# Splitting an expert's gated rows earlier, and another order for the last norm, in an expert layer on one core

## The chip, the cores and the metric

The kernel runs on one core of a Trainium2 chip. The metric is the device time of that core for one execution, in microseconds (us). A core has TensorE (PE, matrix products, with its weight loads shown as PEld), VectorE (DVE), ScalarE (ACT), GpSimd (POOL) and SyncE (SP, which here issues the transfers). Each has its own list of instructions and runs it in order; semaphores hold one back until another has delivered. The time is that of the last core to end, here the only one.

## The reference, cut to what matters

The input is 256 tokens of width 1024 in float32. Two layers are computed: retention and a dense SwiGLU, then stick-breaking attention and an expert SwiGLU. The change touches only the expert layer and the norm behind it:

```python
def moe_swiglu(x, w_router, w_in, w_out):          # 256 tokens, 8 experts, hidden width 3584
    logits = (xt @ w_router).astype(jnp.float32)
    top_val, top_idx = lax.top_k(logits, 2)
    top_w = jax.nn.softmax(top_val, axis=-1)
    gates = sum over the 2 choices of one_hot(top_idx) * top_w
    for e in range(8):
        y = y + gates[:, e:e + 1] * swiglu(xt, w_in[e], w_out[e])
...
# every sub-layer: x <- layer_norm(alpha * x + f(x)); here f is the experts' sum
```

where `swiglu(x, w_in, w_out)` splits `x @ w_in` into gate and up and gives `(silu(gate) * up) @ w_out`.

## The kernel before, in words

Up to about 530 us run the retention layer, the dense SwiGLU, the attention and the router; nothing in them changes but line numbers. Then come the eight experts, where the change lies.

An expert works only on the tokens that chose it, up to CAP = 96 rows in three groups of 32. A one-hot matrix (L801) selects them, and a matmul with it (`pgx`, L817) gathers them, transposed, into `xg` (L826). The hidden width of 3584 is worked in two units: u = 0 with 2048 columns, u = 1 with 1536. For each unit the order in the code (`experts`) is: the gate projection (`gemm_e`, matmuls on L1102), its Silu on ScalarE (L1173), at u = 1 the work between experts (below), the up projection, the product with up (L1192) and its transpose (L1194) on VectorE, and then the down projection of the unit before this one (`down`). So the down projection that finishes an expert's rows runs in the next expert's u = 0, behind that unit's gate and up.

When an expert's rows are finished, `rows_of` copies them out of PSUM (`po`) into `y`: twelve copies of 32x256, the eight of the first two groups on ScalarE and the four of the third on VectorE. They are kept in `done`. The work between experts comes at the next u = 1, after the gate: `scatter` multiplies the rows by their gates and adds them to the residual `xa`. Because TensorE takes the rounded type fp32r, the gated rows are split in two parts: `yh` (ScalarE, L1155) is the gated row rounded, `yl` (VectorE, L1156) what the rounding lost. For each half of the columns (n) and each half of the tokens (t), two matmuls with the transposed one-hot matrix `gT` (L1159 with `yh`, L1160 with `yl`) put the rows in their places, and VectorE adds the result (L1161). Behind it `slots` prepares `gT` and the gates `gs` of the expert in work (transposes and products on TensorE into `pgt`, L1085 and L1087, copies on ScalarE), and the next expert's rows are gathered. Then follows the up projection.

The third group of 32 rows is worked last in a branch that TensorE alone takes (`by_need`), since some experts have at most 64 rows.

All expert weights stream from memory through fourteen 1 MB buffers (`raw`). SyncE issues the load of a buffer (L213) when TensorE has read it for the last time, in the order in which TensorE takes them; at most eight are on their way. Nothing else sets the order: it is the order of the code on each engine, with semaphores between.

After the last expert come its down projection, `scatter` once more, this time with the sums of the norm behind each addition (`stats`, L477), and then a test whether any expert had more than 96 rows (`tc.If(most[0] > CAP)`, L1227). If so, a second pass of all experts runs, several thousand instructions that lie in the program between the test and what follows; with these inputs it isn't taken, and every engine jumps over it. Behind it the last norm: the sums are combined (`mv`, L455), GpSimd computes the reciprocal of the deviation (`rs`, L456 and L457) and `nmr` (L484); for the tokens t = 0 VectorE subtracts the mean (L488, `centre`) and scales (L492, `scale`), for t = 1 ScalarE normalises (L498) and the gain and bias (L502, L503, `affine`) are applied by GpSimd to the first half of the columns and by VectorE to the second. SyncE stores four blocks (L1235).

## Time and profile before

| what | us |
|---|---|
| three runs | 1427.40, 1422.75, 1426.74 (median 1426.74) |
| the profiled execution's own time | 1422.93 |
| its span, first to last instruction | 1421.1 |
| mean granted TensorE clock, share of full speed | 0.974 |
| TensorE busy | 1349.7 (95%) |
| VectorE, ScalarE, GpSimd busy | 443.4, 314.2, 58.5 |

The profiled execution lasts 1.8 us longer than its span. Its own time is 3.8 us below the median of the three runs. Times in rows are us from the start of the span. [...] A line number is that of the kernel before unless the text says otherwise; the changed file's lines stand one to seven further down.

### The profile page before, as it was taken

The numbers are of one execution on the slowest core, as the hardware profiler recorded it, in microseconds if no ns is written. First come the engines' busy times: TensorE is split into PE (matmuls) and PEld (weight loads), VectorE is DVE, ScalarE is ACT, GpSimd is POOL, SyncE is SP. The second block draws the span as 40 slices with busy tenths as digits, with TensorE's granted clock in tenths as the row PEclk, the third lists the DMA queues.
The fourth block names the chain that finished last, engine by engine and source line by source line (L and its number), as shares of the span: only waits on it lengthen the run. The fifth ranks groups of instructions, "written<-read, shape, count | busy, mean of one in ns | idle before, by whom it ended". The sixth has DMA issues, their size and how long they took to land. (4 is left out here: it accounts for less than half of the span.)

```text
span 1421.1 us, 29884 instructions
## 1 busy us (share of the span) xinstructions
PE 1349.7 (95%) x13608; PEld 842.3 (59%) x13608; DVE 443.4 (31%) x617; ACT 314.2 (22%) x466; POOL 58.5 (4%) x80
## 2 busy tenths in 40 slices
PE   9999999999999999987989999999999999999894
PEld 7888879999989863533524444454444453443442
DVE  6746667555566570101201200200200200200204
ACT  5544425444447520001000000100100100100101
POOL 0212110000010020000000000000000000000001
PEclk9999999999999999999999999999999999999997
DMA  9864536655586356999999999989999999999960
GB/s 338 296 210 151 175 119 238 205 180 182 144 243 241 139 223 202 406 418 412 411 419 412 412 418 410 405 341 413 411 418 413 411 402 414 411 418 414 412 271 33
DMA packets 137251, 447.36 MB, mean 315 GB/s; under 512 B 9088, under 2 KB 56976, under 8 KB 120720
## 3 DMA queue, kind: packets, MB, share of 16 engines
q1 hardware_dynamic: 136144, 442.01, 80.9%
q0 software_dynamic: 960, 3.15, 0.7%
q8 instruction: 122, 2.00, 0.6%
q14 instruction: 25, 0.20, 0.0%
HBM read 444.08 MB, written 1.05 MB: 313 GB/s over the span
## 5 line engine op out<-in xcount | busy, mean ns | idle before, releaser
L1102 PE MATMUL pe<-raw,xg 128*32 128x512 f32 (+1 forms) x5304 | 513.3, 543 | 21.4 <-DMA raw<-in_moe_w_in_dram 9.6
L1102 PEld LDWEIGHTS pe<-raw,xg 128*32 128x32 f32 x5304 | 185.5, 110 | 339.6 <-issue 305.3
L1102 PE MATMUL po<-raw,hT 128*32 128x256 f32 x4544 | 249.9, 379 | 5.8 <-DMA raw<-in_moe_w_out_dram 3.3
L265 DVE TENSOR_TENSOR w<-raw,w 128x1024 fp32r<-128x1024 f32 x162 | 198.1, 1234 | 143.8 <-ACT w L264 139.8
L1102 PEld LDWEIGHTS po<-raw,hT 128*32 128x32 f32 x4544 | 158.0, 110 | 100.8 <-issue 7.4
L264 ACT CAST w<-raw 128x1024 fp32r<-128x1024 f32 x162 | 168.2, 1047 | 134.3 <-issue 32.1
L1192 DVE TENSOR_TENSOR hs<-hs,pe 128x512 f32<-128x512 f32 (+1 forms) x48 | 29.1, 620 | 384.0 <-PE pe L1102 382.6
L1173 ACT ACTIVATE hs<-pe 128x512 f32<-128x512 f32 (+1 forms) x48 | 25.4, 543 | 507.5 <-PE pe L1102 507.5
L393 PE MATMUL pf<-xT_h,w 128*128 128x256 f32 x448 | 126.9, 283 | 0.0
L395 PE MATMUL pf<-xT_l,w 128*128 128x256 f32 x448 | 126.2, 282 | 0.0
L394 PE MATMUL pf<-xT_h,w 128*128 128x256 f32 x448 | 126.1, 281 | 0.0
L1194 DVE STREAM_TRANSPOSE hT<-hs 128x512 f32<-128x512 f32 (+1 forms) x48 | 27.2, 617 | 230.0 <-PE po L1102 125.0
L393 PEld LDWEIGHTS pf<-xT_h,w 128*128 128x128 f32 x448 | 84.4, 188 | 0.3
L394 PEld LDWEIGHTS pf<-xT_h,w 128*128 128x128 f32 x448 | 84.4, 188 | 0.3
L395 PEld LDWEIGHTS pf<-xT_l,w 128*128 128x128 f32 x448 | 84.4, 188 | 0.0
L1146 ACT COPY y<-po 32x256 f32<-32x256 f32 x64 | 23.3, 364 | 258.4 <-PE po L1102 257.7
L456 POOL TENSOR_SCALAR rs<-mv 128x1 f32<-128x1 f32 x16 | 5.6, 350 | 1292.4 <-DVE mv L455 1284.5
L368 PE MATMUL pv<-w,xT_l 128*128 128x512 f32 x96 | 38.4, 400 | 0.0
L369 PE MATMUL pv<-w,xT_h 128*128 128x512 f32 x96 | 37.9, 395 | 0.0
L370 PE MATMUL pv<-w,xT_h 128*128 128x512 f32 x96 | 37.9, 395 | 0.0
L1156 DVE SCALAR_TENSOR_TENSOR yl<-y,gs,yh 96x512 fp32r<-96x512 f32 x16 | 11.9, 744 | 82.9 <-ACT yh L1155 82.8
L393 PE MATMUL pq<-xT_h,w 128*128 128x256 f32 x128 | 36.3, 283 | 0.0
(208 smaller groups left out, 1274.1 us busy)
## 6 DMA issues: line engine op xcount, KB each, us to landing
raw<-in_moe_w_in_dram SPq DMA_DIRECT2D x128, 1024.0 KB, 18.9
raw<-in_moe_w_out_dram SPq DMA_DIRECT2D x112, 1024.0 KB, 18.4
raw<-in_moe_w_in_dram SPq DMA_DIRECT2D x128, 768.0 KB, 15.2
raw<-in_ret_w_in_dram SPq DMA_DIRECT2D x22, 1024.0 KB, 9.1
raw<-in_ffn_w_in_dram SPq DMA_DIRECT2D x20, 1024.0 KB, 5.1
raw<-in_ffn_w_out_dram SPq DMA_DIRECT2D x11, 1024.0 KB, 5.0
raw<-in_ret_w_out_dram SPq DMA_DIRECT2D x8, 1024.0 KB, 5.0
raw<-in_sb_w_kv_dram SPq DMA_DIRECT2D x4, 1024.0 KB, 5.3
```

Of the source, the lines that this page charges most:

```text
L264: nc.scalar.copy(hv, v)
L265: nc.vector.tensor_sub(lv, v, hv.bitcast(F32))
L368: nc.tensor.matmul(o, sl, mh, start=first, stop=False)
L369: nc.tensor.matmul(o, sh, mh, start=False, stop=False)
L370: nc.tensor.matmul(o, sh, ml, start=False, stop=last)
L393: nc.tensor.matmul(o, lo[:, k, :], xT_h[:, k, :], start=(k == 0), stop=False)
L394: nc.tensor.matmul(o, h[:, k, :], xT_h[:, k, :], start=False, stop=False)
L395: nc.tensor.matmul(o, h[:, k, :], xT_l[:, k, :], start=False, stop=(k == KD - 1))
L1102: nc.tensor.matmul(ov, lhs[r], w, start=first and not (shared and r == 1), stop=last, skip_group_check=True)
L1173: nc.scalar.activation(hs[:, r, :], pg[r], AF.Silu)
L1192: nc.vector.tensor_mul(hs[:, r, :], hs[:, r, :], pu[r])
L1194: nc.vector.transpose(hT[:, r].rearrange("p k s -> p (k s)"), hs[:, r, :])
```

## The change

The split into `yh` and `yl` moves from `scatter` into `rows_of`, so it is issued right behind the copies of the finished rows; each of its four results has a tile of its own (t0 to t3), where two tiles were used twice before. The copies of the third group alternate between ScalarE and VectorE. The reciprocal deviation of the last norm is computed ahead of the test, for t = 0 first. The branch gets a label, and an announcement of its likely outcome is issued on all engines but TensorE ahead of the last down projection. In the last norm GpSimd applies no gain and bias any more: VectorE does it for both halves of t = 1, behind the scaling of t = 0, and ScalarE's normalisation is issued first.

```diff
--- before.py
+++ after.py
@@ -18,6 +18,7 @@
 AX = mybir.AxisListType
 PSUM = bass.MemoryType.PSUM
 PE = mybir.EngineType.PE
+ENGINES = [getattr(mybir.EngineType, e) for e in ("Activation", "DVE", "PE", "Pool", "SP")]
 
 P = 128
 S = 256
@@ -1138,26 +1139,28 @@
         a, b = wtile("po"), wtile("po")
         return [a[:, :256], a[:, 256:], b[:, :256]]
 
-    def rows_of(po):
+    def rows_of(po, gs):
 
         y = mp2.tile([P, D], F32, tag="y", name=nm("y"))
         for r in range(NB):
             for c in range(4):
-                (nc.scalar.copy if r < 2 else nc.vector.tensor_copy)(
+                (nc.scalar.copy if r < 2 or c % 2 == 0 else nc.vector.tensor_copy)(
                     y[r * 32:(r + 1) * 32, c * 256:(c + 1) * 256], po[r][c * 32:(c + 1) * 32])
-        return y
-
-    def scatter(y, gT, gs, norm=None):
-
+        out_ = []
         for n in range(2):
-            yh = mp.tile([P, 512], FR, tag="t0", name=nm("yh"))[:CAP]
-            yl = mp.tile([P, 512], FR, tag="t1", name=nm("yl"))[:CAP]
+            yh, yl = [mp.tile([P, 512], FR, tag=f"t{2 * n + i}", name=nm("y"))[:CAP] for i in range(2)]
             nc.scalar.activation(yh, y[:CAP, half(n)], AF.Copy, scale=gs[:CAP])
             nc.vector.scalar_tensor_tensor(yl, y[:CAP, half(n)], gs[:CAP], yh.bitcast(F32), OP.mult, OP.subtract)
+            out_.append((yh, yl))
+        return out_
+
+    def scatter(rows, gT, norm=None):
+
+        for n in range(2):
             for t in range(2):
                 p = wtile("psc")
-                nc.tensor.matmul(p, gT[:CAP, t, :], yh, start=True, stop=False)
-                nc.tensor.matmul(p, gT[:CAP, t, :], yl, start=False, stop=True)
+                for i in range(2):
+                    nc.tensor.matmul(p, gT[:CAP, t, :], rows[n][i], start=(i == 0), stop=(i == 1))
                 nc.vector.tensor_add(xa[:, t, half(n)], xa[:, t, half(n)], p)
                 if norm is not None:
                     norm[t].stats(n)
@@ -1197,12 +1200,16 @@
                         po = new_po()
                     down(s, *pend[0], po, pend[1] == 0, pend[1] == 1, third[e - (u == 0)])
                     if pend[1] == 1:
-                        done = (rows_of(po), *sl)
+                        done = (rows_of(po, sl[1]), sl[0])
                 pend = ((hT, n // P), u)
             if e + 1 < NE:
                 xg = nxt
+        if most is not None:
+            tc.mark_branch_hint_location("more", 0, engines=[e for e in ENGINES if e != PE])
         down(s, *pend[0], po, False, True, third[NE - 1])
-        scatter(rows_of(po), *sl, norm)
+        scatter(rows_of(po, sl[1]), sl[0], norm)
+        for t in range(2):
+            norm[t].rstd(t == 1)
 
     norm = [Norm(t, [], xa[:, t, :]) for t in range(2)]
     for t in range(2):
@@ -1224,7 +1231,7 @@
         g = one_hot(0, pos)
         experts(st2, pos, g, gather(g), norm)
 
-    with tc.If(most[0] > CAP):
+    with tc.If(most[0] > CAP, label="more"):
         more(p2)
         with tc.If(most[0] > 2 * CAP):
             nc.vector.tensor_scalar(p2, p2, float(CAP), None, OP.subtract)
@@ -1234,17 +1241,14 @@
     def store(t, n):
         nc.sync.dma_start(out[0, t * P:(t + 1) * P, half(n)], xa[:, t, half(n)])
 
-    for t in (1, 0):
-        norm[t].rstd(t == 1)
+    norm[1].normalise(0, 1)
     for n in range(2):
         norm[0].centre(n)
-    norm[1].normalise(0, 1)
-    norm[1].affine(0, nc.gpsimd, nc.gpsimd)
     for n in range(2):
         norm[0].scale(n)
         store(0, n)
-    norm[1].affine(1, nc.vector, nc.vector)
-    for n in (1, 0):
+    for n in range(2):
+        norm[1].affine(n, nc.vector, nc.vector)
         store(1, n)
```

On ScalarE, at the rows of the last expert but one (`po` holds the finished rows, `hs` is the next unit's Silu, `pgt` what `slots` computed), the program before has:

```order
L1146 COPY y_11626<-po_11015 32x256 [waits PE_49]
L1146 COPY y_11626<-po_11015 32x256 x7
L1173 ACTIVATE hs_11639<-pe_11640 128x384 [waits DVE_49,PE_49]
L1118 UNCONDITIONAL_BRANCH
L1173 ACTIVATE hs_11639<-pe_11641 128x384 [waits PE_49]
L1173 ACTIVATE hs_11639<-pe_11642 128x384 [waits PE_49]
L1155 ACTIVATE yh_11759<-y_11626,gs_10857 96x512 [waits DVE_49,Activation_49]
L1155 ACTIVATE yh_11771<-y_11626,gs_10857 96x512 [waits DVE_49,PE_49]
L1090 CAST gT_11788<-pgt_11783 128x256 [waits PE_49]
L1092 COPY gs_11790<-pgt_11783 128x1 [waits DVE_49]
```

and the changed program has, where the two split results `yh` are both named `y`:

```order
L1147 COPY y_11626<-po_11015 32x256 [waits PE_49]
L1147 COPY y_11626<-po_11015 32x256 x7
L1147 COPY y_11626<-po_11016 32x256 [waits PE_49]
L1147 COPY y_11626<-po_11016 32x256 [waits DVE_49]
L1152 ACTIVATE y_11639<-y_11626,gs_10857 96x512 [waits Activation_49]
L1152 ACTIVATE y_11643<-y_11626,gs_10857 96x512 [waits DVE_49]
L1176 ACTIVATE hs_11647<-pe_11648 128x384 [waits PE_49]
L1119 UNCONDITIONAL_BRANCH
L1176 ACTIVATE hs_11647<-pe_11649 128x384 [waits PE_49]
L1176 ACTIVATE hs_11647<-pe_11650 128x384 [waits PE_49]
L1091 CAST gT_11788<-pgt_11783 128x256 [waits PE_49]
L1093 COPY gs_11790<-pgt_11783 128x1 [waits DVE_49]
```

The two multiplications with the gates stood behind the three Silus of the next u = 1 and waited there for `yl` of the earlier half and for TensorE; they now follow the copies, ahead of the Silus, and two copies more stand in front of them.

On GpSimd, from the load of the largest row count to the end (`nmax` is that count, `x_87` and the like earlier tiles of the residual, `neghalf` the exponent), the program before has:

```order
L1181 TENSOR_LOAD nmax [waits DVE_49]
L1227 COMPARE_AND_BRANCH
L1229 COMPARE_AND_BRANCH
L1229 UNCONDITIONAL_BRANCH x2
L1227 UNCONDITIONAL_BRANCH
L456 TENSOR_SCALAR rs_27137<-mv_27136 128x1 [waits DVE_49]
L457 TENSOR_TENSOR rs_27137<-rs_27137,neghalf 128x1 [waits Pool_49]
L484 TENSOR_SCALAR nmr_27141<-mv_27136,rs_27137 128x1 [waits Pool_49]
L456 TENSOR_SCALAR rs_27144<-mv_27143 128x1 [waits DVE_49]
L457 TENSOR_TENSOR rs_27144<-rs_27144,neghalf 128x1 [waits Pool_49]
L502 TENSOR_TENSOR xa<-xa,gbt 128x512 [waits DMAHW5_49,Activation_49]
L503 TENSOR_TENSOR xa<-xa,gbt 128x512 [waits DMAHW7_49,Pool_49]
```

and the changed program, up to its jump:

```order
L1184 TENSOR_LOAD nmax [waits DVE_49]
L457 TENSOR_SCALAR rs_12293<-mv_12292 128x1 [waits DVE_49]
L458 TENSOR_TENSOR rs_12293<-rs_12293,neghalf 128x1 [waits Pool_49]
L457 TENSOR_SCALAR rs_12298<-mv_12297 128x1 [waits DVE_49]
L458 TENSOR_TENSOR rs_12298<-rs_12298,neghalf 128x1 [waits Pool_49]
L485 TENSOR_SCALAR nmr_12302<-mv_12297,rs_12298 128x1 [waits Pool_49]
L1234 COMPARE_AND_BRANCH
```

Before, the jump came right behind the load of the count, long ahead of the end, and the five instructions of the norm behind it. Now the five stand between the load and the jump, and nothing of GpSimd's follows the jump in the path that is taken.

## Rows read from the trace of the kernel before

**Rows 1.** Waits, whole span: engine, line, waited for; us in total, times, longest.

```profile
PE psc L1159 <- ACT yh L1155: 15.7, 16, 1.8
...
PE psc L1160 <- DVE yl L1156: 6.2, 16, 1.6
...
PE pe L1102 <- DMA raw<-in_moe_w_in_dram: 9.6, 15, 2.0
```

**Rows 2.** Page part 2, slices of 35.5 us: memory traffic.

```profile
GB/s 338 296 210 151 175 119 238 205 180 182 144 243 241 139 223 202 406 418 412 411 419 412 412 418 410 405 341 413 411 418 413 411 402 414 411 418 414 412 271 33
```

**Rows 3.** Timeline, TensorE: start, length, instruction, count, [idle before <- releaser].

```profile
578.79 0.41 PE L1085 MATMUL pgt<-ident,g 128*128 128x128 f32 x2 [0.17 <-PEq L1118]
...
579.47 2.80 PE L817 MATMUL pgx<-x,g 128*32 128x256 f32 x48
...
729.56 28.53 PE L1102 MATMUL pe<-raw,xg 128*32 128x512 f32 x264 [0.56 <-DMA raw<-in_moe_w_in_dram]
...
1319.42 15.69 PE L1102 MATMUL pe<-raw,xg 128*32 128x384 f32 x192 [1.50 <-DMA raw<-in_moe_w_in_dram]
...
1337.43 0.40 PE L1159 MATMUL psc<-yh,gT 96*128 96x512 f32 x1
1337.66 0.40 PE L1160 MATMUL psc<-yl,gT 96*128 96x512 f32 x1
```

**Rows 4.** The load issued at 1308.64: where it starts, issue to landing.

```profile
L213 SPq DMA_DIRECT2D raw<-in_moe_w_in_dram x1: 328/328/328, 1308.6 to 1308.6; - x1
...
DMA to landing us min/median/max: 15.9/15.9/15.9
```

**Rows 5.** Windows: stretch, length; PE, PEld, DVE, ACT, POOL busy; clock, DMA share, GB/s.

```profile
650.00:660.00 10.00, 7.51 (x128) 3.59 (x120) 0.00 (x0) 0.46 (x2) 0.00 (x0) 1.00 1.03 414
920.00:930.00 10.00, 10.00 (x131) 4.18 (x124) 1.11 (x2) 0.00 (x0) 0.00 (x0) 1.00 0.76 312
930.00:940.00 10.00, 10.00 (x175) 5.67 (x168) 0.56 (x1) 0.00 (x0) 0.00 (x0) 1.00 0.77 296
1050.00:1335.00 285.00, 273.86 (x3348) 125.50 (x3348) 35.74 (x67) 21.35 (x49) 0.00 (x0) 0.97 1.01 412
1335.10:1342.28 7.18, 4.63 (x16) 3.10 (x15) 4.07 (x6) 1.82 (x3) 0.00 (x0) 0.79 1.02 412
1342.28:1359.64 17.36, 17.36 (x194) 6.22 (x197) 1.11 (x2) 0.43 (x2) 0.00 (x0) 0.89 1.02 408
```

**Rows 6.** Page part 5, copies of finished rows on ScalarE: busy, mean ns, idle before.

```profile
L1146 ACT COPY y<-po 32x256 f32<-32x256 f32 x64 | 23.3, 364 | 258.4 <-PE po L1102 257.7
```

**Rows 7.** Timeline, all engines, after the last down projection.

```profile
1397.11 1.74 DVE L1146 COPY y<-po 32x256 f32<-32x256 f32 x4 [15.01 <-PE po L1102]
1398.05 0.72 ACT L1155 ACTIVATE yh<-y,gs 96x512 fp32r<-96x512 f32 x1 [2.68 <-DVE y L1146]
...
1400.23 0.69 DVE L1161 TENSOR_TENSOR xa<-xa,psc 128x512 f32<-128x512 f32 x1 [0.59 <-PE psc L1160]
...
1406.53 0.69 DVE L477 BATCH_NORM_STATS2 st<-xa 128x6 f32<-128x512 f32 x1
1409.52 0.28 DVE L455 BATCH_NORM_AGGREGATE mv<-st 128x2 f32<-128x12 f32 x2 [2.29 <-DVEq L1227]
1409.81 0.23 POOL L456 TENSOR_SCALAR rs<-mv 128x1 f32<-128x1 f32 x1 [877.82 <-DVE mv L455]
...
1411.77 0.56 POOL L457 TENSOR_TENSOR rs<-rs,neghalf 128x1 f32<-128x1 f32 x1
...
1412.36 3.43 DVE L492 SCALAR_TENSOR_TENSOR xa<-xa,rs,gbt 128x512 f32<-128x512 f32 x2 [1.11 <-POOL rs L457]
...
1416.43 0.69 DVE L503 TENSOR_TENSOR xa<-xa,gbt 128x512 f32<-128x512 f32 x1
```

**Rows 8.** Line 1227, the jump over the second pass, on ScalarE.

```profile
L1227 ACTq COMPARE_BRANCH  x1: 50/50/50, 1400.5 to 1400.5; - x1
L1227 ACTq EVENT_SEMAPHORE  x1: 17/17/17, 1403.1 to 1403.1; - x1
```

## The prediction, on record before the changed kernel ran

> **What bounds the kernel now.** I read the page first. The memory traffic [rows 2] is full, 400 to 420 GB/s, from slice 17 on, where the experts' weights stream; one slice, the 27th, shows 341. TensorE is busy 95% all the same, so the next view was the waits: with its last weights TensorE hardly waits, 9.6 us in 15 waits on this line, while each expert's scatter makes it wait for the split rows, 15.7 us for `yh` and 6.2 us for `yl`, over eight scatters [rows 1]. TensorE's timeline tells when each of the two limits holds. Until 729.56 it waits for weights chunk by chunk; that row is the last such wait [rows 3]. (The wait of 1.50 us at 1319.42 bears the same name but stands behind a skipped third group, a jump; that gate's first weights had landed by then, since its eighth and last was issued at 1308.64 and took 15.9 us [rows 4], and chunks land about 1.9 us apart, 768 KB at 412 GB/s [rows 5].) So in the first experts memory is the limit, and from there on TensorE is, by a growing margin. Where TensorE lags far enough, buffers come free late and memory pauses: 312 and 296 GB/s in 920 to 940 against 412 to 414 elsewhere [rows 5], which is (1-312/414) x 10 + (1-296/414) x 10 = 5.3 us of transfer lost. The chain that sets the end is therefore TensorE from about 730 on, and the tail behind 1397.11, which I read as a list in order of time [rows 7].

> **Term 1, the experts up to the last gate.** The split no longer waits for the Silus behind a gate, so a scatter's eight matmuls find their operands there. They save at least their mean wait, 21.9/8 = 2.7 us an expert, and five scatters with it lie between 729.56 and the last gate: 13.7 us. TensorE can't take all of it, because weights become the limit again. The last gate's eighth chunk lands at 1308.64 + 15.9 = 1324.5 [rows 4]; TensorE reaches it after 120 of the gate's 192 matmuls (eight for each chunk and group; the first chunk with three groups, six more with two), at 1319.42 + 120 x 0.0817 = 1329.2 [rows 3]. That is 4.7 us of room. If TensorE frees buffers in time, the lost transfer comes back as well, between 0 and 5.3 us; I take 5.0, because two or three scatters, 5.4 to 8.1 us, stand between 729.56 and 920. Together 9.7 us, less than the 13.7 that TensorE offers, so the weights decide the term: 9.7, with ends 4.7 and 10.0.

> What the move adds costs nothing here. On ScalarE ten copies of 0.364 [rows 6] and two products of 0.72 [rows 7], 5.1 us, now stand ahead of the next Silus; they run beside the next gate, 15.69 us [rows 3], or 136/192 of it, 11.1, where the third group is skipped. On VectorE two copies go and the two `yl` come earlier. Their cover would be gone only if that gate were under 5.1 us. The copies of the third group hand over between the two engines, three times 0.07 us (the gap between the second copy's end, 1397.11 + 2 x 0.435, and `yh` at 1398.05 [rows 7]); the same gate hides that. The selection of the next expert's rows stands behind the four additions on VectorE as before, and those come earlier.

> **Term 2, the last scatter and the last up projection.** From the last gate's end, 1335.10, to the up projection's start it is 7.18 us, with TensorE busy 4.63 of them at a granted clock of 0.79; the up projection takes 17.36 us at 0.89 [rows 5]: 24.54 together. The clock fell in a stretch in which TensorE stood idle a third of the time. The same eight matmuls without a wait follow one another every 0.23 us at full clock (1337.43 to 1337.66 [rows 3]): 1.84; the transposes of the one-hot matrix take 0.68 up to what follows them (578.79 to 579.47 [rows 3]); 0.1 for the four small products behind. The up projection has the last gate's shape and takes 15.69 at full clock [rows 3]. Sum 18.3, so 6.2 us less. If the clock falls all the same, the eight matmuls take 3.7 and the up projection its 17.36; with 0.8 between, 21.9, and the gain is 2.6. I take 6.2, since little idle time is left ahead of the fall.

> **Term 3, the tail.** Counted from 1397.11 [rows 7]. The third group's copies alternate: 0.36 + 0.07 + 0.44 + 0.07 + 0.36 = 1.30 until ScalarE is free for `yh`; it is done at 2.0, the second at 2.7; the two `yl` on VectorE, taken as long as `yh`, end at about 3.6. Then VectorE has four additions and four statistics of 0.69: 9.1. Before, the last statistics ended at 1407.22, that is 10.1. Next the combined statistics, 0.14 each, and GpSimd's chain, which took 2.5 us from 1409.81 to 1412.33; it begins at 9.3 and ends at 11.9. Before, a jump lay between, and VectorE lost 2.29 us on it [rows 7]; now the chain is ahead of the jump, and the jumps come next. What an announced jump costs no row shows: an unannounced one took ScalarE 2.6 us, from 1400.5 to 1403.1, while the compare itself took 0.05 [rows 8]. So it costs 0 to 2.6; I take 0.2, three branch instructions and a compare at 0.05, because the announcement comes a whole down projection ahead. This decides, as GpSimd's jump now stands behind its chain, where before it had passed it 877.82 us before its chain began [rows 7], and both `scale` and `normalise` wait for GpSimd's count behind the jump. At 12.1 VectorE begins two scalings and four steps of gain and bias, 6 x 0.69 = 4.1 (the 3.43 of the two scalings before lay beside GpSimd's work on the same tile; the single step of VectorE's at 1416.43 took 0.69), so 16.2. ScalarE's normalisation, two steps that I take as long as `yh`, runs beside the scalings. From VectorE's last instruction to the end of the span it was 1421.10 - 1417.12 = 3.98, which stays. The tail is then 20.2 instead of 23.99: 3.8 less. The two steps that VectorE takes over from GpSimd, 1.4, are in it.

> **The sum.** 9.7 + 6.2 + 3.8 = 19.7 us. The profiled execution took 1422.93, so its like would take 1403.2. The median of the runs shown lies 3.8 higher, and so does the forecast for a median: 1426.74 - 19.7 = 1407.0.

> **Rivals.**

> (a) The announcement does nothing. Then ScalarE's, VectorE's and GpSimd's jumps take 2.6 us each; GpSimd's is the last, from 11.9 to 14.5, and the tail takes 22.6, a gain of 1.4 instead of 3.8. For it: no row shows an announcement at work, and the jump goes over thousands of instructions. Against it: the engines pass it with nothing else to do. 1426.74 - 17.3 = 1409.4. [...]

> (b) The lost transfer is not regained and the clock falls as before: 4.7 + 2.6 + 3.8 = 11.1, so 1415.6. For it: memory paused because of how far TensorE lagged over several experts, and only two or three scatters come before that place. With (a) on top it is 1418.0.

> (c) Everything gained in the experts is given back to waits for weights, for instance because the transfers of the last experts themselves come later: the tail alone, 3.8, so 1422.9. Against it: the 4.7 us between landing and use are there in the trace.

> (d) Slower. In the later experts TensorE would wait for weights again as it did before 730. If the granted clock falls with these waits, every matmul stretches. The stretch from 1050 to 1335 takes 285 us at 0.97 [rows 5]; each hundredth of clock is worth 2.85 us, so the gain is used up and 4.3 us lost when the mean clock falls by 24/2.85 = 8.4 hundredths, to 0.886; that gives 1431. Against it stands 650 to 660, where TensorE waited a quarter of the time for weights, busy 7.51 of 10.00, at a granted clock of 1.00 [rows 5]. [...]

> **How the numbers follow.** Forecast 0.46, its own range 1402 to 1411 (term 1 a little short, the median's scatter); (a) 0.20; (b) 0.21; (c) 0.08; (d) 0.05. A measurement of this kernel can tell about 0.3%, 4.3 us, from no change. Faster by more than that are the forecast, (a) and (b), 0.87; within it (c), 0.08; slower (d), 0.05. The range from 1400 to 1419 holds the first three, with (a) and (b) together at its upper end, and a term 2 or a jump slightly better than taken at its lower.

> **What would show it.** Term 1: in the waits, TensorE's wait for `yh` and `yl` shrinks from 21.9 us to that of the last scatter alone, some 2 us; its waits for `raw` grow from 9.6 and appear in the last experts; the 27th slice's 341 GB/s is gone; the last gate ends near 1325. Term 2: from that gate's end to the up projection about 2.6 us, the clock there above 0.95, the up projection near 15.7. Term 3: statistics end 9.1 us after the down projection, GpSimd's jump is short, and the last instruction of VectorE starts some 15.5 us after it. It is wrong if the scatters still wait, if memory shows the same pause, or if the clock in 1050 to 1335 falls below 0.97.

## The result and the profile after

| | median, us | range | runs |
|---|---|---|---|
| before | 1426.56 | 1422.75 to 1427.40 | 4 |
| changed | 1405.49 | 1404.64 to 1405.70 | 4 |

The ratio is 0.9851, 95% interval 0.9839 to 0.9863: 21.1 us less. The forecast was 1407.0, range 1400 to 1419.

The page of the changed kernel, its span and the slices of 35.1 us for TensorE's clock (tenths) and memory:

```profile
span 1403.6 us, 29908 instructions
...
PEclk9999999999999999999999999999999999999997
...
GB/s 336 283 212 173 162 126 236 191 186 185 176 184 296 125 250 203 300 417 414 410 419 413 412 417 414 412 406 415 412 415 414 408 415 411 407 412 417 396 394 71
```

The 27th slice, 341 GB/s in [rows 2], is 406 now.

TensorE's waits in the changed kernel (waited for: us in total, times, longest), where both split parts are named `y`:

```profile
PE pe L1103 <- DMA raw<-in_moe_w_in_dram: 14.3, 26, 2.1
...
PE po L1103 <- DMA raw<-in_moe_w_out_dram: 13.4, 20, 2.1
...
PE psc L1163 <- ACT y L1152: 2.1, 1, 2.1
...
PE psc L1163 <- DVE y L1153: 0.2, 1, 0.2
```

The waits for `yh` and `yl`, 15.7 and 6.2 [rows 1], are 2.1 and 0.2, one each: the scatter behind the very last down projection. The wait for gate and up weights has grown from 9.6 [rows 1] to 14.3, and for the down weights there are 20 waits, 13.4 us, where there were five, 3.3 us. TensorE's timeline shows where:

```profile
580.89 0.41 PE L1086 MATMUL pgt<-ident,g 128*128 128x128 f32 x2 [0.17 <-PEq L1119]
...
731.78 28.53 PE L1103 MATMUL pe<-raw,xg 128*32 128x512 f32 x264 [0.55 <-DMA raw<-in_moe_w_in_dram]
...
1032.58 1.93 PE L1103 MATMUL po<-raw,hT 128*32 128x256 f32 x32 [0.49 <-DMA raw<-in_moe_w_out_dram]
```

```profile
1320.87 1.50 PE L1103 MATMUL pe<-raw,xg 128*32 128x384 f32 x16 [0.38 <-DMA raw<-in_moe_w_in_dram]
1322.76 6.01 PE L1103 MATMUL pe<-raw,xg 128*32 128x384 f32 x72 [0.39 <-DMA raw<-in_moe_w_in_dram]
...
1331.32 15.69 PE L1103 MATMUL pe<-raw,xg 128*32 128x384 f32 x192
...
1368.43 15.81 PE L1103 MATMUL po<-raw,hT 128*32 128x256 f32 x288 [0.70 <-DVE hT L1197]
```

The row at 731.78 answers to the one at 729.56 [rows 3]: up to there both kernels wait for weights, chunk by chunk. The kernel before hardly waited so again: besides the wait of 1.50 us at 1319.42 that the prediction explains, there is one of 0.37 us at 1105.85, which the prediction passed over. The changed one does from 1032.58 on, and in the last gate it waits for single chunks at 1320.87 and 1322.76. That gate ends at 1328.77, the eight scatter matmuls stand right behind it, and the up projection starts at 1331.32. The same in windows (columns as in [rows 5]):

```profile
920.00:930.00 10.00, 10.00 (x160) 6.00 (x155) 1.66 (x3) 0.00 (x0) 0.00 (x0) 1.00 1.01 406
930.00:940.00 10.00, 10.00 (x193) 7.27 (x188) 0.00 (x0) 0.00 (x0) 0.00 (x0) 1.00 1.02 422
1050.00:1335.00 285.00, 267.06 (x3322) 119.01 (x3326) 35.28 (x64) 25.77 (x60) 0.00 (x0) 1.00 1.01 410
1328.77:1331.32 2.55, 2.55 (x15) 2.13 (x14) 1.85 (x4) 0.49 (x1) 0.00 (x0) 1.00 1.02 418
1331.32:1346.83 15.51, 15.51 (x194) 6.27 (x197) 1.75 (x4) 0.43 (x2) 0.00 (x0) 1.00 1.02 409
```

The memory pause at 920 to 940 is gone (406 and 422 for 312 and 296 [rows 5]). The scatter stretch takes 2.55 us at a clock of 1.00 where it took 7.18 at 0.79, the up projection 15.51 at 1.00 where it took 17.36 at 0.89.

The tail of the changed kernel, all engines:

```profile
1384.30 0.36 ACT L1147 COPY y<-po 32x256 f32<-32x256 f32 x1 [1.76 <-PE po L1103]
...
1392.59 0.69 DVE L478 BATCH_NORM_STATS2 st<-xa 128x6 f32<-128x512 f32 x1
...
1393.48 0.23 POOL L457 TENSOR_SCALAR rs<-mv 128x1 f32<-128x1 f32 x1 [860.53 <-DVE mv L456]
...
1395.01 0.92 POOL L458 TENSOR_TENSOR rs<-rs,neghalf 128x1 f32<-128x1 f32 x1
...
1396.39 1.41 DVE L493 SCALAR_TENSOR_TENSOR xa<-xa,rs,gbt 128x512 f32<-128x512 f32 x2 [0.87 <-POOLq L1234]
...
1399.77 0.69 DVE L504 TENSOR_TENSOR xa<-xa,gbt 128x512 f32<-128x512 f32 x1
```

It lasts from 1384.24, the end of the last down projection, to 1403.6. VectorE's scalings take 1.41, where they took 3.43 beside GpSimd [rows 7]. The jump over the second pass, engine by engine (x count: ns, first and last start):

```profile
L1234 ACTq COMPARE_BRANCH  x1: 68/68/68, 1386.0 to 1386.0; - x1
L1234 ACTq EVENT_SEMAPHORE  x1: 17/17/17, 1386.9 to 1386.9; - x1
...
L1234 DVEq COMPARE_BRANCH  x1: 84/84/84, 1393.3 to 1393.3; - x1
L1234 DVEq EVENT_SEMAPHORE  x1: 21/21/21, 1393.9 to 1393.9; - x1
L1234 POOLq COMPARE_BRANCH  x1: 59/59/59, 1396.0 to 1396.0; - x1
L1234 POOLq EVENT_SEMAPHORE  x1: 17/17/17, 1396.3 to 1396.3; - x1
```

From compare to the first event behind it ScalarE needs 0.9 us (2.6 before [rows 8]), VectorE 0.6, GpSimd 0.3.

### The profile page after: what moved, and what is told of

Its sections match the earlier page's. It is cut to its first block, busy times and chain, and to the rows that moved or that the text cites. A ratio compares the mean times of both kernels' runs of the same rounds, so it can differ in the third digit from the quotient of the medians.

```text
span 1403.6 us, 29908 instructions
## 1 busy us (share of the span) xinstructions
PE 1329.6 (95%) x13608; PEld 841.2 (60%) x13608; DVE 434.7 (31%) x603; ACT 319.9 (23%) x482; POOL 55.8 (4%) x78
## 5 line engine op out<-in xcount | busy, mean ns | idle before, releaser
L1103 PE MATMUL pe<-raw,xg 128*32 128x512 f32 (+1 forms) x5304 | 515.0, 542 | 26.6 <-DMA raw<-in_moe_w_in_dram 14.3
L1103 PEld LDWEIGHTS pe<-raw,xg 128*32 128x32 f32 x5304 | 190.2, 110 | 342.0 <-issue 293.2
L1103 PE MATMUL po<-raw,hT 128*32 128x256 f32 x4544 | 252.7, 380 | 16.1 <-DMA raw<-in_moe_w_out_dram 13.4
L1103 PEld LDWEIGHTS po<-raw,hT 128*32 128x32 f32 x4544 | 161.3, 110 | 110.7 <-DMA raw<-in_moe_w_out_dram 22.7
L1147 ACT COPY y<-po 32x256 f32<-32x256 f32 x80 | 29.0, 363 | 276.5 <-PE po L1103 267.0
L1164 DVE TENSOR_TENSOR xa<-xa,psc 128x512 f32<-128x512 f32 x32 | 20.1, 681 | 71.8 <-PE psc L1163 71.8
## 6 DMA issues: line engine op xcount, KB each, us to landing
raw<-in_moe_w_in_dram SPq DMA_DIRECT2D x128, 768.0 KB, 15.2
```

The costliest lines, as they stand in the source:

```text
L1103: nc.tensor.matmul(ov, lhs[r], w, start=first and not (shared and r == 1), stop=last, skip_group_check=True)
L1147: (nc.scalar.copy if r < 2 or c % 2 == 0 else nc.vector.tensor_copy)(y[r * 32:(r + 1) * 32, c * 256:(c + 1) * 256], po[r][c * 32:(c + 1) * ...
```

## The experiments

The changed kernel's three terms are first taken apart: the tail's part and the rows' part each alone, then single steps of each. All times are medians. The experiments ran in four groups, each with the kernel before beside it: it took 1426.48 (the first two and the runs without announcement and with old copies), 1425.94 (the late splits), 1424.51 (GpSimd's gain and bias, another last norm) and 1426.89 (the last two). Differences to the changed kernel are to 1405.49 unless said otherwise. The spread of one kernel's runs is 1 to 6 us, so differences below about 1 us are read from traces, not from times.

**The rows' part alone.** The changed kernel with the announcement taken out and the old end of `trunk_kernel`:

```diff
-        for t in range(2):
-            norm[t].rstd(t == 1)
...
-    norm[1].normalise(0, 1)
+    for t in (1, 0):
+        norm[t].rstd(t == 1)
     for n in range(2):
         norm[0].centre(n)
+    norm[1].normalise(0, 1)
+    norm[1].affine(0, nc.gpsimd, nc.gpsimd)
...
```

> The kernel before with the rows' part of the change alone: split at the end of the down projection, third group's copies alternating, old tail (no announcement, reciprocal deviation behind the test, GpSimd's gain and bias). Theory: terms 1 and 2 and the copies' part of the tail, 14.7 + 0.9 = 15.6 us less than before: about 1411. Rival (the tail carries more than I counted, the experts less): above 1413.

Measured: 1408.92 (1407.53 to 1410.22; ratio to before 0.9879, interval 0.9863 to 0.9896), 17.6 us less than before, 2 more than expected; the interval, 14.8 to 19.5, holds the 15.6. In its trace the copies begin at 1383.64 and the span ends at 1406.5: a tail of 22.9, 1.1 less than before (0.9 expected).

**The tail's part alone.** The kernel before with the announcement, the early reciprocal deviation and the new end; rows split late.

```diff
+        if most is not None:
+            tc.mark_branch_hint_location("more", 0, engines=[e for e in ENGINES if e != PE])
         down(s, *pend[0], po, False, True, third[NE - 1])
         scatter(rows_of(po), *sl, norm)
+        for t in range(2):
+            norm[t].rstd(t == 1)
...
```

> The kernel before with the tail's part of the change alone: announcement, reciprocal deviation ahead of the test, last norm without GpSimd's elementwise work; rows split late as before. Theory: the experts' trace stays that of before, the tail is 2.9 to 3.8 us shorter: 1423.2. Rival: nothing, since GpSimd's jump now stands in the path: 1426.

Measured: 1421.72 (ratio 0.9969, interval 0.9957 to 0.9982), 4.8 less. In its trace the last down projection's copies begin on VectorE at 1399.48 and the span ends at 1419.9: 20.4, against 24.0 before, so 3.6 us, which the interval of the runs, 2.6 to 6.1, holds. With the 1.1 of the rows' part it makes the 4.7 by which the changed kernel's whole tail is shorter. The rival, no gain, falls.

**Late split behind the last gate only.** This and the next three keep the changed kernel and split the rows late, in the scatter and with two tiles used twice as before, for chosen experts:

```diff
+        if late:
+            return y, gs
...
-                        done = (rows_of(po, sl[1]), sl[0])
+                        done = (rows_of(po, sl[1], e == 7), sl[0])
```

> The changed kernel, but the rows that are scattered behind the last gate are split late, as before (in the scatter, behind that gate's Silus, two tiles used twice); all other scatters as changed. Theory: this takes back term 2 alone. The last gate ends at 1328.8 as in the changed kernel, the way from there to the up projection grows from 2.6 to about 7.2 and the clock in the up projection falls to 0.89: +6.3, 1411.8. Rival (the clock's part belongs to what came before the gate, not to this scatter): +4.6, 1410.1.

Measured: 1411.30, +5.8. Windows of its trace, from the last gate's end to the up projection, and the up projection:

```profile
1329.02:1336.18 7.16, 4.59 (x16) 3.07 (x15) 4.07 (x6) 1.82 (x3) 0.00 (x0) 0.82 1.02 414
1336.18:1353.78 17.60, 17.60 (x193) 6.30 (x196) 1.11 (x2) 0.43 (x2) 0.00 (x0) 0.88 1.02 408
```

The last gate ends where it ended in the changed kernel (1329.02 for 1328.77). The wait and the clock both come back: 7.16 + 17.60 = 24.76 against 18.06, of which 4.6 lies in the scatter and 2.1 in the slower up projection. A late split brings back two things at once, the later place and the two tiles used twice, and no run parts them: in this trace TensorE waits 1.21 and 0.28 us ahead of the first half's products, and 0.58 and 0.48 ahead of the second's, whose tiles are used again.

**Late split behind the gates of experts 1 to 6.** `e < 7` in place of `e == 7`; the experts count from 0.

> The changed kernel, but the rows scattered behind the gates of the experts 1 to 6 are split late; the scatter behind the last gate and the final one are as changed. Theory: this takes back term 1 alone: the memory pause at 920 to 940 returns, TensorE hardly waits for weights after 730, and the last gate ends as late as before: +6.3 (the two traces' difference at the last gate's end) to +8.4 (the same without the 2.1 us by which the changed kernel's trace had started the experts later): 1411.8 to 1413.9. Rival (term 1 comes from the last scatters only): under 1408.

Measured: 1416.25 (1413.59 to 1418.32), +10.8, more than expected. The last gate begins at 1321.36 and ends at 1337.05, 8.3 us after that of the changed kernel, or 9.4 counted from the first expert's transposes (579.79 here, 580.89 there). The traced run, 1413.59, is the fastest of the five. The gate's row, and this kernel's waits:

```profile
1321.36 15.69 PE L1103 MATMUL pe<-raw,xg 128*32 128x384 f32 x192 [1.19 <-DMA raw<-in_moe_w_in_dram]
...
PE psc L1174 <- ACT y L1168: 11.8, 12, 1.6
...
PE pe L1103 <- DMA raw<-in_moe_w_in_dram: 8.3, 12, 2.0
...
PE psc L1174 <- DVE y L1169: 3.8, 12, 0.5
...
PE po L1103 <- DMA raw<-in_moe_w_out_dram: 2.4, 4, 0.8
```

The twelve waits of six scatters, 11.8 and 3.8 us, are back, and those for weights are down to 8.3 and 2.4. Memory pauses again, 345 and 244 GB/s in 920 to 930 and 930 to 940. The rival that only the last scatters count falls.

**One late split, at expert 5.**

> The changed kernel with one late split, behind the gate of expert 5. Theory: the changed kernel's TensorE waits for weights in every expert after that, so the 3 to 5 us that the late split costs TensorE there are taken from those waits: no change, 1405.5, with TensorE's waits for weights a few us shorter. Rival (every late split costs its own time): 1409 to 1410.

Measured: 1405.22 (1402.89 to 1407.06), no change. The late scatter is there, and so is its price: from that gate's end to the up projection TensorE takes 11.9 us (1113.02 to 1124.91), in the changed kernel 6.1 (1112.86 to 1118.97). Four waits for the split rows take 2.6 of it, where the changed kernel waits 0.9 for the one-hot matrix; the other 4.1 of the 5.8 more go to a lower clock, 0.89 in 1110 to 1120 and 0.77 in 1120 to 1130; the 48 matmuls of the gathering alone take 5.01 us, in the changed kernel 2.80. The waits for weights in its trace show who pays:

```profile
PE pe L1103 <- DMA raw<-in_moe_w_in_dram: 13.9, 26, 1.6
...
PE po L1103 <- DMA raw<-in_moe_w_out_dram: 9.8, 14, 1.6
```

Weights are waited for 23.7 us in all, where the changed kernel waited 27.7. By 1253.79 TensorE has made up its lag: the matmul there starts at 1253.61 in the changed kernel. The last gate ends at 1328.92, 0.15 later. So the 5.8 us that this late scatter takes on TensorE cost nothing here, where weights are late anyway.

**Two late splits, at experts 2 and 3.**

> The changed kernel with two late splits, behind the gates of experts 2 and 3, at about 789 and 903 us, ahead of the place where memory paused before. Theory: TensorE lags 6 to 9 us more there and frees buffers late, memory pauses again and loses up to 5 us, and as weights are the limit afterwards this lasts to the end: 1410. Rival: the waits for weights from 1032 on take it up as in the run with expert 5: 1405.5.

Measured: 1409.47, +4.0. Windows around the old pause:

```profile
910.00:920.00 10.00, 9.00 (x69) 5.56 (x73) 4.62 (x11) 1.16 (x3) 0.00 (x0) 0.66 1.03 412
920.00:930.00 10.00, 10.00 (x128) 4.18 (x124) 0.37 (x2) 0.00 (x0) 0.00 (x0) 1.00 0.87 355
930.00:940.00 10.00, 10.00 (x160) 5.25 (x156) 1.66 (x3) 0.00 (x0) 0.00 (x0) 1.00 0.61 228
```

Memory pauses again: 355 and 228 GB/s, which against 414 loses 1.4 + 4.5 = 5.9 us. In 1050 to 1335 it then moves 414 GB/s, where the changed kernel has 410, which makes up some 2.8 of them (285 us x 4/412). The clock in 910 to 920, behind the late scatter, is 0.66. In its last gate this kernel waits for single chunks as the changed one does, and that gate ends at 1332.25, 3.5 later. Two late scatters here cost 4.0 us, one at expert 5 nothing: what lasts is the lost transfer that isn't made up, not TensorE's own time.

**Without the announcement.** The two lines with `mark_branch_hint_location` are taken out of the changed kernel.

> The changed kernel without the announcement of the branch; the order of the tail is the changed one. Theory (the prediction's): an unannounced jump takes 2.6 us on every engine; GpSimd's stands last, so scale and normalise begin 2.3 us later (2.6 for 0.3): 1407.8. Rival: GpSimd's jump goes over 14 instructions of its own only and takes 0.3 announced or not; then VectorE's jump grows from 0.6 to about 2.8, subtracting the mean (1.42) ends at 1397.7 instead of 1395.5 on the scale of the changed kernel's trace, and the scalings start 1.3 late: 1406.8. A third: the announcement does nothing anywhere, 1405.5.

Measured: 1405.91 (1405.36 to 1407.66), 0.4 more, less than runs can tell. The trace tells the three theories apart, first the jumps, then the first scaling:

```profile
L1232 DVEq COMPARE_BRANCH  x1: 72/72/72, 1393.0 to 1393.0; - x1
L1232 POOLq COMPARE_BRANCH  x1: 45/45/45, 1394.9 to 1394.9; - x1
L1232 POOLq EVENT_SEMAPHORE  x1: 17/17/17, 1395.3 to 1395.3; - x1
L1232 DVEq EVENT_SEMAPHORE  x1: 21/21/21, 1395.9 to 1395.9; - x1
```

```profile
1394.32 0.56 POOL L458 TENSOR_TENSOR rs<-rs,neghalf 128x1 f32<-128x1 f32 x1
...
1397.37 1.41 DVE L493 SCALAR_TENSOR_TENSOR xa<-xa,rs,gbt 128x512 f32<-128x512 f32 x2
```

GpSimd's jump takes 0.4 without an announcement. VectorE's takes 2.9, ends at 1395.9, and the subtraction of the mean behind it lasts until 1397.4, where the scaling begins. From the end of the last statistics to the first scaling it is 4.4 us, in the changed kernel 3.1: 1.3, the second theory's figure. From the last down projection to the end of the span it is 1.1 more.

**The third group's copies on VectorE alone, as before.**

```diff
-                (nc.scalar.copy if r < 2 or c % 2 == 0 else nc.vector.tensor_copy)(
+                (nc.scalar.copy if r < 2 else nc.vector.tensor_copy)(
```

> The changed kernel with all four copies of the third group on VectorE, as before. Theory: only the last one shows, 4 x 0.44 = 1.74 instead of the alternating chain; the first yh starts at 0.94 after two copies in the old way (VectorE) and at 1.24 in the changed one, while the first yl waits for VectorE's fourth copy until 1.74 instead of 1.99 when yh is done: within 0.3 us of the changed kernel, 1405.5. Rival: alternating saves the 0.5 us by which the chain is shorter: 1406.0.

Measured: 1404.5, the median of four runs from 1403.67 to 1405.11; a fifth took 4807.81, for which I have no cause, and is left out. From the first of these copies to the end of the span it is 19.1 us, in the changed kernel 19.3. Alternating is worth nothing.

**Gain and bias of one half given back to GpSimd.**

```diff
-        norm[1].affine(n, nc.vector, nc.vector)
+        norm[1].affine(n, *([nc.vector] * 2 if n else [nc.gpsimd] * 2))
```

> The changed kernel with gain and bias of t = 1, first half, given back to GpSimd. Theory: GpSimd's two steps begin behind ScalarE's first normalisation (1397.2 on the scale of the changed kernel's trace) and stretch VectorE's scalings from 1.4 to 3.4 us; VectorE then has two steps instead of four: its last ends at 1396.4 + 3.4 + 1.4 = 1401.2 instead of 1400.5, so the tail is 0.7 us longer: 1406.2. Rival: without stretching, VectorE would end 1.4 us earlier and the tail be shorter: 1404.6.

Measured: 1405.80 (1404.92 to 1406.44), +0.3; by the ratio to the kernel before beside it, 0.9867 for 0.9851, it is +2.3, so the runs alone don't settle it. The trace has 0.8 us where 0.7 were expected (from the end of the last statistics 11.1 us to the end of the span, changed 10.3), but elsewhere than expected:

```profile
1395.97 1.41 DVE L493 SCALAR_TENSOR_TENSOR xa<-xa,rs,gbt 128x512 f32<-128x512 f32 x2 [0.88 <-POOLq L1234]
...
1396.87 1.64 POOL L503 TENSOR_TENSOR xa<-xa,gbt 128x512 f32<-128x512 f32 x1 [0.98 <-ACT xa L499]
1397.52 1.53 DVE L503 TENSOR_TENSOR xa<-xa,gbt 128x512 f32<-128x512 f32 x1
...
1399.09 1.63 DVE L504 TENSOR_TENSOR xa<-xa,gbt 128x512 f32<-128x512 f32 x1
```

The scalings stay at 1.41; VectorE's own gain and bias, 0.69 each alone, take 1.53 and 1.63 beside GpSimd's. Two steps of VectorE beside GpSimd cost 3.2 us, four without it 2.8.

**Another last norm.** The reciprocal deviation of t = 0 goes ahead of the last addition, and VectorE centres and scales both t:

```diff
                     norm[t].stats(n)
+                    if n == 1:
+                        norm[t].rstd()
...
-    norm[1].normalise(0, 1)
-    for n in range(2):
-        norm[0].centre(n)
+    for t in range(2):
+        for n in range(2):
+            norm[t].centre(n)
```

> The changed kernel with another last norm: the reciprocal deviation of t = 0 is issued right behind its own last statistics, ahead of the last addition for t = 1; both t are centred and scaled by VectorE (nothing by ScalarE, no nmr on GpSimd). Theory: GpSimd's chain for t = 0 lies beside VectorE's last two steps, its chain behind the last statistics is 0.8 to 1.5 us instead of 2.8; behind the jump VectorE has eight steps of 0.68 without a wait: its last ends 6.1 us behind the last statistics instead of 7.2: 1404.4. Rival: GpSimd's small instructions stretch beside VectorE's centring, as from 2.1 to 2.8 us when the announcement brought that centring forward, and VectorE waits for the second deviation: 1405.5.

Measured: 1403.25 (1402.28 to 1404.46), 2.2 less; by the ratio to the kernel before beside it, 0.9846 for 0.9851, only 0.7. VectorE's last ends 6.2 us behind the last statistics (expected 6.1, changed kernel 7.2):

```profile
1392.52 0.69 DVE L478 BATCH_NORM_STATS2 st<-xa 128x6 f32<-128x512 f32 x1
...
1394.03 2.74 DVE L489 SCALAR_TENSOR_TENSOR xa<-xa,mv,gbt 128x512 f32<-128x512 f32 x4 [0.57 <-DVEq L1234]
1396.69 2.73 DVE L493 SCALAR_TENSOR_TENSOR xa<-xa,rs,gbt 128x512 f32<-128x512 f32 x4
```

The eight steps follow without a wait. The combining of t = 0 now stands ahead of the last statistics and moves them back a little, so the whole tail is 18.7 against 19.4 us.

**Both, beside the changed kernel.** The norm of the last run with the old copies, and the changed kernel itself once more:

> The interleaved last norm of the run before, and the third group's four copies all on VectorE again. Theory: the interleaved norm is worth the 0.6 us that its trace shows behind the last down projection, and the copies nothing (19.1 and 19.3 us of tail in the two traces): 0.6 to 1 us below the changed kernel run beside it. Rival: the difference of the run before to the changed kernel (2.2 us between runs of different calls) was the spread of the runs, and this one is level with the changed kernel.

> The changed kernel once more, as the measure for the run beside it: 1405.5, as before, since nothing in it differs.

Measured: 1404.02 (1402.87 to 1404.79; ratio to before 0.9835) and 1405.63 (1402.52 to 1406.76; ratio 0.9845), five runs each. The first is 1.6 us faster by the medians, but the two ranges overlap; its trace has 18.4 us of tail for 19.4. By the ratio to the kernel before it is the fastest version here, by less than these runs can prove. The second run of the changed kernel also shows how much a trace's start varies: the same transposes as at 580.89 above stand here at

```profile
579.60 0.41 PE L1086 MATMUL pgt<-ident,g 128*128 128x128 f32 x2 [0.17 <-PEq L1119]
```

and its last gate ends 1.4 us earlier, at 1327.34.

## Why the prediction was right, step by step

| | predicted | the two traces | one part alone, by medians |
|---|---|---|---|
| term 1, up to the last gate's end | 9.7 | 6.3; 8.4 from the first expert's transposes | 10.8 (taken back: experts 1 to 6 late) |
| term 2, scatter and up projection | 6.2 | 24.54 - 18.06 = 6.5 | 5.8 (taken back: last gate late) |
| term 3, tail | 3.8 | 4.7 | 4.8 (put in: tail's part, without the rows' 1.1; trace 3.6) |
| sum | 19.7 | 17.5; 19.6 from those transposes | the whole change: 21.1 |

That 19.6 meets 19.7 is in part luck: term 1 came out 1.3 smaller, terms 2 and 3 together 1.2 larger. The interval of the ratio, 19.5 to 23.0 us, holds both; where the 1.5 between 19.6 and 21.1 lies, no trace shows.

**What bounds.** The reading held: TensorE was the limit from 730 to the end of the last gate, and in that stretch memory is now, from 1032 on. The single late split that costs nothing shows it most directly.

**Term 1** rested on two numbers. The 4.7 us between landing and use are used up: the last gate waits for chunks. The 5.0 for the memory pause was too large; 4.1 came. From the end of the chunk wait at 729.56 to the landing of the last gate's eighth chunk, 1324.5, it was 595.0 us; now it is 590.9, from 731.78 to 1322.7 (issued at 1307.47, 15.2 until it landed). The pause itself is gone, and bringing it back with two late splits costs 4.0. The reason given for the 5.0, two or three scatters between 729.56 and 920, holds: two were enough in that run. The last gate ends at 1328.8, not near 1325. Of that, 2.1 us stand in the trace by the first expert's transposes, 578.79 [rows 3] against 580.89, ahead of anything that the change touches in the experts (1.85 of it already at the first expert's gate, 530.83 against 532.68); the changed kernel's second profile has them at 579.60. Over all profiles of this study they lie between 578.79 and 581.34, so the trace of before was the earliest, which fits its own time below its median. Why the start varies is open. Of the last 1.3 us, 0.9 are the transfer that did not come. It fits the 410 GB/s in 1050 to 1335 for 412 [rows 5], which is 1.4 us over 285, as far as figures rounded to 1 GB/s tell; in 1050 to 1320, too, it is 410 for 412. Why the stream is slower there no run tests. The 13.7 that TensorE offers counted the waits alone; with the lower clock the late scatter at expert 5 cost it 5.8. As the weights decide the term, that changed nothing.

**Term 2** came as worked out, 2.55 + 15.51 against 18.3, the clock included. The late split behind the last gate alone brings back the idle time and, with it, the clock of 0.82 in the scatter and 0.88 in the up projection; without the idle time the fall is gone, as taken. The 3.7 for the eight matmuls under a fallen clock, part of rival (b)'s 2.6, was my estimate, 1.84 doubled; the trace of before has them 0.43 us apart (1340.22 to 1340.65) at a granted clock of 0.50 in 1340 to 1341, which makes 3.4.

**Term 3.** Most steps fit to 0.1 us from the first copy at 1384.30: statistics end at 9.0 (9.1), the scaling begins at 12.1 (12.1), VectorE ends at 16.2 (16.2). Three things were not as I put them:

- That the 3.98 "stays" failed: it is 3.14 now. Before, the two stores of t = 1 were issued with the one that waits for VectorE's last step first, so two issues followed that step, at 1417.2 and 1417.6; the changed code orders n = 0, 1, and one follows it, at 1400.5. I had read the order in the diff and not priced it. That is 0.4 to 0.5 of the 0.84; the rest is open.
- "This decides", said of the announcement, failed in its reason. GpSimd's jump is short without an announcement too: 0.4 unannounced, 0.3 announced. GpSimd has only 14 instructions of its own in the second pass, ten of them steps of the norm that the change itself puts there; that this is the reason fits, but no run varies it. The price of 0.2 came near by luck. What the announcement shortens is VectorE's jump (2.9 to 0.6) and ScalarE's (2.4, from 1385.9 to 1388.3, to 0.9), and VectorE's then stands ahead of the centring. The 2.6 was ScalarE's [rows 8]; for GpSimd, whose instructions I had not counted, it was no more than an estimate.
- The chain on GpSimd takes 2.8, not 2.5. Its small steps stretch beside VectorE's centring: the second power takes 0.92 there, at 1395.01, and 0.56 without the announcement, at 1394.32, when VectorE still jumps. The other way round, VectorE's two scalings took 3.43 beside GpSimd's gain and bias [rows 7] and take 1.41 without them. Why the two slow each other no run shows.

**Alternating copies** had no price of their own in the sum but were part of its 9.1; they are worth nothing (19.1 and 19.3 us), since VectorE's fourth copy lay beside ScalarE's first product.

**The rivals.** (a), announcement without effect, would have given 1409.4; it gives 1405.9, since the rival took GpSimd's jump for 2.6. (b), pause and clock as before, and (c), all given back, are refuted by the windows. (d): the clock in 1050 to 1335 is 1.00 with the waits for weights, 0.97 before; those waits, at most 0.7 us each in this stretch, did not lower it. But what (d) feared was seen once, in the first experts, behind the longest wait for weights of this trace:

```profile
641.84 5.34 PE L1103 MATMUL pe<-raw,xg 128*32 128x512 f32 x32 [2.13 <-DMA raw<-in_moe_w_in_dram]
```

The clock is 0.61 in 642 to 644 and 0.54 in 644 to 646. Behind the wait of 2.06 us at 711.80, and behind the one of 1.96 at 639.59 in the kernel before, it stayed at 1.00; what decides is open. So (d) was refuted for the short waits of the later experts.

## What to carry to other kernels

Where two limits lie close together, work out how far the one that isn't binding now is behind (here the time between a weight's landing and its use, and the transfer lost in pauses): that caps what a change to the other can bring, and it tells which waits are free. Split or prepare an operand as soon as it is ready, on engines that idle then, and not only when it is needed; here some two thirds of the price lay in the scatter that waited and a third in the slower product behind it. Price a jump for each engine by itself (unannounced it took 0.4 us on GpSimd here, 2.4 on ScalarE and 2.9 on VectorE), and before pricing a tail, count the transfers issued behind the last step.
